# Four of eleven down-projection units by a seven-product block scheme

## The chip, the cores and the metric

The kernel runs on one core of a Trainium2 chip. TensorE multiplies matrices into PSUM, VectorE and ScalarE do elementwise work, GpSimd a little of it, and DMA queues bring the weights in from HBM. The metric is the device time of one execution in microseconds. The profile's rows call the engines PE (TensorE; PEld is its loading of the 128x128 operand that it holds), DVE (VectorE), ACT (ScalarE), POOL (GpSimd) and SP (the queue that issues most DMAs).

## The reference

One layer of a decoder on 256 tokens of width 1024: a mixing block (pooling, an mLSTM and block attention), which the change doesn't touch, and then the feed-forward block:

```python
h2 = rmsnorm(x, ln2_g[l])
u = causal_dwconv(h2 @ w_up[l], ffn_conv[l])              # 1024 -> 2 x 2816
x = x + (jax.nn.silu(u[..., :D_FF]) * u[..., D_FF:]) @ w_down[l]   # 2816 -> 1024
```

The change is in the last product, 256 x 2816 by 2816 x 1024, in float32.

## The kernel before, in words

Every float32 product is made as three matmuls in a shorter type (fp32r). Each operand is split into a *high* part, a copy that ScalarE rounds to fp32r, and a *low* part, the rest, that VectorE gets by a subtraction; the matmuls are high x high, high x low and low x high.

The weights come in *units* of 1 MB (128 partitions x 2048 columns) through a ring of four raw buffers; `load` issues the DMA of the unit four ahead as soon as a unit's split is written in program order, and that DMA waits on the queue until the raw buffer has been read. `split` makes a unit's high part (line 184, ScalarE) and low part (line 191, VectorE) in halves of 1024 columns, into rings of four buffers each (`HL_BUFS`); a half can be written only when TensorE is done with the unit four buffers ago.

The up products (units of the gate and value columns, lines 1110 to 1174) end with one of them per 128 rows of the hidden width: `up_sum`, `up_taps`, `up_gate` and `up_out` leave the gated values, transposed, as `a_hi` and `a_lo`: 22 slabs of 128 rows by 256 tokens. In the program's names raw37 to raw47 are the eleven down units 0 to 10.

The down product has eleven units. Unit i holds 256 rows of `w_down`: two row blocks k = 0, 1 of 128, times 1024 columns, which are two halves c = 0, 1 of 512. The tokens are two blocks t = 0, 1 of 128. So a unit is a 2 x 2 block matrix of tokens (t by k) times a 2 x 2 block matrix of weights (k by c): eight block products, each of three matmuls of 128x128 by 128x512, 24 matmuls in all. Four PSUM accumulators (t, c) collect them over the units. `rows_product` (line 849) writes them.

The order is the order of the program on every engine; nothing is moved later. In the loop from line 1189, unit i's matmuls are written together with the split of unit i + 2. The last two units are kept apart: the four accumulators are finished one after the other, added to the residual `xs` by VectorE (line 1184) and written out, the last one in two tails of 256 columns in other PSUM tiles (`tail`), so that little is left after the last matmul.

Of the kernel before, what the change touches and what calls it, by code (L numbers as in the profile page):

```python
# [26 lines left out]
UMAX = 2080  # L27
RAW_BUFS = 4
# [100 lines left out]
def kernel(  # L129
# [22 lines left out]
    def big(name):  # L152
        return tpool.tile([P, D], F32, tag="big", name=name, bufs=3)
# [7 lines left out]
    def aux(shape, name):  # L161
        return psum.tile(shape, F32, tag="aux", name=name, bufs=4)


    hi_t, lo_t, raw_t = {}, {}, {}

    def unit_cols(u):
        return UMAX if u < N_IN and IN_UNITS[u] in ("vi", "of") else 2048

    def load(u):  # L170
        if u >= N_UNITS:
            return
# [4 lines left out]
        nc.sync.dma_start(raw[:, :n], src)

    def split_hi(u, part, parts):
        if u not in hi_t:  # L180
            hi_t[u] = wpool.tile([P, UMAX], F32R, tag="hi", name=f"hi{u}", bufs=HL_BUFS)
        n = unit_cols(u)
        s = slice(part * n // parts, (part + 1) * n // parts)
        nc.scalar.activation(hi_t[u][:, s], raw_t[u][:, s], AF.Copy)  # L184

    def split_lo(u, part, parts):
        if u not in lo_t:
            lo_t[u] = wpool.tile([P, UMAX], F32R, tag="lo", name=f"lo{u}", bufs=HL_BUFS)
        n = unit_cols(u)
        s = slice(part * n // parts, (part + 1) * n // parts)  # L190
        nc.vector.tensor_sub(lo_t[u][:, s], raw_t[u][:, s], hi_t[u][:, s].bitcast(F32))  # L191
# [26 lines left out]
    for a, b in PARTS:  # L218
        c = slice(KT * (a > 0) + S * a, KT + S * b)
# [18 lines left out]
    def hi_lo(hi, lo, src):  # L238
        nc.scalar.activation(hi, src, AF.Copy)  # L239
        nc.vector.tensor_sub(lo, src, hi.bitcast(F32))  # L240
# [13 lines left out]
    h_2 = cpool.tile([P, KT, 2, S], F32R, name="h_2")  # L254
# [582 lines left out]
    acc = {}  # L837

    def rows_product(u, lhs, kk, first, last, t, cs=(0, 1), ks=(0, 1), sub=(0, 512)):
        hw = hi_t[u][:, :2048].rearrange("p (k c) -> p k c", c=D)  # L840
        lw = lo_t[u][:, :2048].rearrange("p (k c) -> p k c", c=D)
        tok = slice(t * P, (t + 1) * P)
        for k in ks:
            st, sp = first and k == 0, last and k == 1
            lh, ll = lhs[0][:, kk + k, tok], lhs[1][:, kk + k, tok]
            for i, (a, b) in enumerate(((lh, hw), (lh, lw), (ll, hw))):
                for c in cs:
                    o, n = 512 * c + sub[0], sub[1] - sub[0]
                    nc.tensor.matmul(acc[t, c][:, :n], a, b[:, k, o:o + n], start=st and i == 0, stop=sp and i == 2)  # L849
# [22 lines left out]
    for q in range(4):  # L872
        f = [("f", 0), ("f", 1)] if q == 0 else [("f", q + 1)]
# [39 lines left out]
    h = 0  # L913
# [47 lines left out]
    for t in range(NT):  # L961
# [7 lines left out]
        dst = (slice(None), slice(2, 4), slice(t * P, (t + 1) * P))  # L969
# [53 lines left out]
    for n in range(4, n_end):  # L1023
# [30 lines left out]
    up_r, y_t = {}, {}  # L1054
# [88 lines left out]

    def up_gate(i):
        nc.scalar.activation(y_t[i, 0], y_t[i, 0], AF.Silu)  # L1145
        nc.vector.tensor_mul(y_t[i, 1], y_t[i, 0], y_t[i, 1])  # L1146

    def up_out(i):
        hi_lo(a_hi[:, i, :], a_lo[:, i, :], y_t[i, 1])

    for i in range(2, NPAIR + 1):
        u = U_UP + i
        if i == 2:
            up(i, (0,))
            up_rows_t(0)
            up_rows_t(1)
            up(i, (1,))
        elif i < NPAIR:
            up(i)
        for m in (0, 1) if i == 2 else (i - 1,):  # L1160
            if m > 1:
                up_sum(m)
            if i < NPAIR and m:
                split_hi(u + 2, 0, 2)
            up_last(m)
            if i < NPAIR and m:
                split_hi(u + 2, 1, 2)
            if m > 1:
                split_lo(u + 1, 1, 2)
            up_taps(m)  # L1170
            up_gate(m)
            if i < NPAIR and m:
                split_lo(u + 2, 0, 2)
            up_out(m)

    def down(i, t, cs=(0, 1), span=(0, N_DOWN - 1), sub=(0, 512)):
        if i == 0:
            for c in cs:
                acc[t, c] = aux([P, 512], f"dn{t}{c}")
        rows_product(U_DOWN + i, (a_hi, a_lo), 2 * i, i == span[0], i == span[1], t, cs, sub=sub)  # L1180

    def finish(t, c, sub=(0, 512), queue=nc.sync):
        s = slice(c * 512 + sub[0], c * 512 + sub[1])
        nc.vector.tensor_add(xs[:, t, s], acc[t, c][:, :sub[1] - sub[0]], xs[:, t, s])  # L1184
        if queue is not None:
            queue.dma_start(out[t * P:(t + 1) * P, s], xs[:, t, s])

    last = (N_DOWN - 2, N_DOWN - 1)
    for i in range(last[0]):
        down(i, 0)  # L1190
        split(U_DOWN + i + 2, 0)
        down(i, 1, (0,))
        down(i, 1, (1,), (0, last[0] - 1))
        split(U_DOWN + i + 2, 1)
    finish(1, 1, queue=None)
    for i in last:
        down(i, 0)
    for c in range(2):
# [100 lines left out]
```

## Time and profile before

| | us |
|---|---|
| median of 3 runs | 305.64 (305.23 to 306.33) |
| the profiled execution's own time | 305.76 |
| its span, first to last instruction | 304.0 |
| TensorE busy in it | 298.2 |
| VectorE busy | 235.6 |
| ScalarE busy | 196.3 |
| first matmul of the down product starts | 239.56 |
| last addition of a tail starts | 300.73 |

Times in rows are microseconds from the span's start, durations behind them; a group's row has the busy time and the mean duration in ns. An arrow names what ended the idle time ahead of an instruction. Matmul ends are modelled and overlap the next start; a distance between starts is safer. The share of busy time is an average over stages with different limits: VectorE's 77% is 95% of the up stage (105.52 of 111.60 us from 128.0 to 239.6) and 47% of the down stage (28.92 of 61.10 us).

### The profile page before, as it was taken

The page shows a single profiled execution, that of the slowest core. Times are in us where ns is not written, and L with a number is a line of the kernel's source. Part 1 is how long each engine was busy: PE and PEld are TensorE (multiplying, and loading weights), DVE is VectorE, ACT ScalarE, POOL GpSimd, SP SyncE. Part 2 cuts the span into 40 slices and gives each one's busy share as a digit, 9 for nine tenths or more (in the row PEclk, how much of TensorE's full clock was granted, in tenths as well). Part 3 has the DMA queues.
Part 4 walks back from the last instruction along what each step waited for, and adds up shares of the span by engine and source line. Part 5 has one row for each costly group of instructions (what it writes and reads, how often), then busy time and mean ns, then how long its engine had stood idle before and what let it go on. Part 6 is the DMA issues. An engine that isn't in the chain of part 4 may idle for free.

```text
span 304.0 us, 4444 instructions
## 1 busy us (share of the span) xinstructions
PE 298.2 (98%) x1635; PEld 250.6 (82%) x1635; DVE 235.6 (77%) x467; ACT 196.3 (65%) x373; POOL 10.7 (4%) x30
## 2 busy tenths in 40 slices
PE   7999999999999999999999999999999999999995
PEld 3899888788778778888888888888888888888884
DVE  2866999999876667769999999999999986435122
ACT  3775977779995546868777786777877585234000
POOL 1000104510000000000000000000000000000000
PEclk9999999999999999999999999999999999999999
DMA  7999774033337370343563645545456469500003
GB/s 183 394 417 401 307 274 151 2 126 150 123 156 267 149 277 0 140 138 138 160 251 144 227 190 177 240 148 237 170 188 226 141 196 425 208 0 0 0 2 138
DMA packets 9829, 55.20 MB, mean 182 GB/s; under 512 B 1092, under 2 KB 1872, under 8 KB 3920
## 3 DMA queue, kind: packets, MB, share of 16 engines
q1 hardware_dynamic: 9664, 54.79, 48.6%
q8 instruction: 13, 0.21, 0.3%
q10 hardware_dynamic: 144, 0.13, 0.1%
q14 instruction: 8, 0.07, 0.1%
HBM read 53.86 MB, written 1.05 MB: 181 GB/s over the span
## 4 chain that ended last, share of the span: by engine, by line
PE 83%; DVE 7%; DMA 5%; ACT 2%; issue 1%; SPq 1%; ACTq 0%
PE up L1119 24%; PE dn L849 19%; PE up L1120 13%; PE wo L849 7%; DMA raw<-in_w 4%; DVE lo L191 3%; PE of L475 2%; DMA x_t<-in_xt 2%; PE upr L1065 1%; PE V L460 1%; PE upr L1064 1%; PE V L461 1%; PE upr L1066 1%; PE V L462 1%; PE B L460 1%; PE B L462 1%
## 5 line engine op out<-in xcount | busy, mean ns | idle before, releaser
L191 DVE TENSOR_TENSOR lo<-raw,hi 128x1024 fp32r<-128x1024 f32 (+2 forms) x100 | 114.2, 1163 | 24.1 <-ACT hi L184 23.9
L1119 PE MATMUL up<-h,hi 128*128 128x512 f32 x320 | 112.5, 396 | 0.0
L184 ACT ACTIVATE hi<-raw 128x1024 fp32r<-128x1024 f32 (+2 forms) x100 | 97.4, 999 | 21.2 <-PE dn L849 18.0
L1120 PE MATMUL up<-h,lo 128*128 128x256 f32 x320 | 90.1, 282 | 0.0
L1119 PEld LDWEIGHTS up<-h,hi 128*128 128x128 f32 x320 | 60.1, 188 | 14.2 <-DVE z L1127 0.2
L1120 PEld LDWEIGHTS up<-h,lo 128*128 128x128 f32 x320 | 60.2, 188 | 0.0
L1140 DVE SCALAR_TENSOR_TENSOR fy<-z,par,fy 128x255 f32<-128x255 f32 (+1 forms) x80 | 33.2, 476 | 0.0
L849 PE MATMUL dn<-hi,a_lo 128*128 128x512 f32 x84 | 29.5, 394 | 0.0
L849 PE MATMUL dn<-hi,a_hi 128*128 128x512 f32 x84 | 29.4, 393 | 0.0
L849 PE MATMUL dn<-lo,a_hi 128*128 128x512 f32 x84 | 29.4, 393 | 0.0
L1133 ACT ACTIVATE fy<-z,par 128x256 f32<-128x256 f32 x40 | 18.2, 502 | 4.3 <-DVE z L1127 4.3
L849 PEld LDWEIGHTS dn<-lo,a_hi 128*128 128x128 f32 x84 | 15.8, 188 | 3.6
L849 PEld LDWEIGHTS dn<-hi,a_lo 128*128 128x128 f32 x84 | 15.8, 188 | 3.6
L849 PEld LDWEIGHTS dn<-hi,a_hi 128*128 128x128 f32 x84 | 15.7, 188 | 3.6
L1145 ACT ACTIVATE fy<-fy 128x256 f32<-128x256 f32 x22 | 9.2, 418 | 12.5 <-DVE fy L1140 12.4
L239 ACT ACTIVATE a_hi<-fy 128x256 fp32r<-128x256 f32 x22 | 9.2, 418 | 10.8 <-DVE fy L1146 10.8
L1127 DVE TENSOR_TENSOR z<-up,zl 128x512 f32<-128x512 f32 x20 | 13.7, 685 | 0.4 <-ACT zl L1125 0.3
L1184 DVE TENSOR_TENSOR xs<-dn,xs 128x512 f32<-128x512 f32 x4 | 2.7, 688 | 14.0 <-PE dn L849 14.0
L1125 ACT ACTIVATE zl<-up 128x512 f32<-128x512 f32 x20 | 11.7, 585 | 1.7 <-PE up L1120 1.5
L1146 DVE TENSOR_TENSOR fy<-fy,fy 128x256 f32<-128x256 f32 x22 | 9.4, 426 | 3.6 <-ACT fy L1145 2.4
L849 PE MATMUL wo<-hi,mix_hi 128*128 128x512 f32 x32 | 11.1, 409 | 0.0
L849 PE MATMUL wo<-lo,mix_hi 128*128 128x512 f32 x32 | 10.6, 393 | 0.0
(270 smaller groups left out, 469.6 us busy)
## 6 DMA issues: line engine op xcount, KB each, us to landing
raw<-in_w SPq DMA_DIRECT2D x46, 1024.0 KB, 4.8
raw<-in_wg SPq DMA_DIRECT2D x2, 520.0 KB, 6.6
xs<-in_x SPq DMA_DIRECT2D x2, 512.0 KB, 9.7
raw<-in_wg SPq DMA_DIRECT2D x3, 260.0 KB, 5.5
x_t<-in_xt SPq DMA_DIRECT2D x3, 256.0 KB, 5.0
mb<-far SPq DMA_DIRECT2D x1, 768.0 KB, 5.5
out_y<-xs SPq DMA_DIRECT2D x3, 256.0 KB, 2.0
par<-in_params SPq DMA_DIRECT2D x1, 337.0 KB
```

The source lines that it names most:

```text
L184: nc.scalar.activation(hi_t[u][:, s], raw_t[u][:, s], AF.Copy)
L191: nc.vector.tensor_sub(lo_t[u][:, s], raw_t[u][:, s], hi_t[u][:, s].bitcast(F32))
L239: nc.scalar.activation(hi, src, AF.Copy)
L849: nc.tensor.matmul(acc[t, c][:, :n], a, b[:, k, o:o + n], start=st and i == 0, stop=sp and i == 2)
L1119: nc.tensor.matmul(ps[:, j], a, h_2[:, k].rearrange("p c t -> p (c t)"), start=k == 0, stop=False)
L1120: nc.tensor.matmul(ps[:, j, :S], b, h_hi[:, k, :], start=False, stop=k == KT - 1)
L1125: nc.scalar.activation(zl, ps[:, :, S:], AF.Copy)
L1127: nc.vector.tensor_add(z, ps[:, :, :S], zl)
L1133: nc.scalar.activation(y_t[i, j], up_t[i][j], AF.Copy, scale=pcol(Q_FC + i + NPAIR * j + 4 * NPAIR))
L1140: nc.vector.scalar_tensor_tensor(y[:, d:], up_t[i][j][:, :S - d], pcol(Q_FC + i + NPAIR * j + 2 * NPAIR * tap), y[:, d:], op0=ALU.mult, op ...
L1145: nc.scalar.activation(y_t[i, 0], y_t[i, 0], AF.Silu)
L1146: nc.vector.tensor_mul(y_t[i, 1], y_t[i, 0], y_t[i, 1])
```

## The change

For units 2, 4, 6 and 8 the 2 x 2 block product is made from seven block products instead of eight. With token blocks A (t by k) and weight blocks B (k by c) the products are

- M1 = A00 B00 and M2 = A01 B10, on blocks as they are;
- M3 on a difference of token blocks and B11; M4 on A11 and a sum of weight blocks;
- M5, M6 and M7 on differences of token blocks and sums of weight blocks.

M2, M3 and M4 go straight into three of the accumulators that the plain units use. M1 and M5, and M6 and M7, get PSUM tiles of their own, in which they add up over the four units; `combine` puts them together once, after unit 8.

Per such unit VectorE forms four sums of weight blocks (`p13`, `p24`, 2048 columns in three instructions) and four differences of token blocks (`sd`, 512 columns in three), and these get high and low parts as well; of the unit's own blocks only B00, B10 and B11 are still split. The gated values of these units are kept in float32 in a new tile `a_sv`, and the parts of the token differences go into `h_2`, which the up products have done with. A unit of this kind takes two of the four buffers of each ring of high and low parts. The loop prepares a unit when the buffers allow it (`ready`), and the matmuls of unit i are no longer written between the two halves of a split.

Diff, cut to its core:

```diff
+SEVEN = (2, 4, 6, 8)
     def up_gate(i):
         nc.scalar.activation(y_t[i, 0], y_t[i, 0], AF.Silu)
-        nc.vector.tensor_mul(y_t[i, 1], y_t[i, 0], y_t[i, 1])
+        y = a_sv[:, slot[i], :] if i in slot else y_t[i, 1]
+        nc.vector.tensor_mul(y, y_t[i, 0], y_t[i, 1])
+        y_t[i, 1] = y
...
+    def three(dst, a, b, start, stop):
+        for n, (x, y) in enumerate(((0, 0), (0, 1), (1, 0))):
+            nc.tensor.matmul(dst, a[x], b[y], start=start and n == 0, stop=stop and n == 2)
...
+    def down_seven(i):
+        if i == SEVEN[0]:
+            for a, b in ((1, 5), (6, 7)):
+                m = psum_u.tile([P, 2, 2 * S], F32, tag="up", name=f"m{a}{b}", bufs=2)
+                m_t[a], m_t[b] = m[:, 0], m[:, 1]
+            m_t[2], m_t[3], m_t[4] = acc[0, 0], acc[0, 1], acc[1, 0]
+        for n, a, b in ((1, token_block(i, 0, 0), weight_block(i, 0)), (2, token_block(i, 1, 0), weight_block(i, 2)),
+                        (3, diff_block(i, 3), weight_block(i, 3)), (5, diff_block(i, 1), sum_block(i, 0)),
+                        (7, diff_block(i, 0), sum_block(i, 1)), (6, diff_block(i, 2), sum_block(i, 2)),
+                        (4, token_block(i, 1, 1), sum_block(i, 3))):
+            own = n not in (2, 3, 4)
+            three(m_t[n], a, b, own and i == SEVEN[0], own and i == SEVEN[-1])
+
+    def diffs(i):
+        n = SEVEN.index(i)
+        v = a_sv[:, 2 * n:2 * n + 2, :].rearrange("p k (t c) -> p (k t) c", c=P)
+        sd = big(f"sd{i}")
+        d = sd[:, :4 * P].rearrange("p (b c) -> p b c", c=P)
+        nc.vector.tensor_tensor(d[:, 0:2, :], v[:, 1:2, :].to_broadcast([P, 2, P]), v[:, 0:4:3, :], op=ALU.subtract)
+        nc.vector.tensor_sub(d[:, 2, :], v[:, 0, :], d[:, 1, :])
+        nc.vector.tensor_sub(d[:, 3, :], v[:, 2, :], d[:, 2, :])
+        s_hl[i] = [h_2[:, 2 * (n % 4) + x].rearrange("p c t -> p (c t)") for x in range(2)]
+        return sd[:, :4 * P]
+
+    def half_hl(h, l, src, s):
+        nc.scalar.activation(h[:, s], src, AF.Copy)
+        nc.vector.tensor_sub(l[:, s], src, h[:, s].bitcast(F32))
+
+    def sums(i):
...
+        p13 = big(f"p13_{i}")
+        nc.vector.tensor_tensor(p13.rearrange("p (b c) -> p b c", c=512), r[:, 0:4:3, :],
+                                r[:, 1:2, :].to_broadcast([P, 2, 512]), op=ALU.add)
+        p24 = big(f"p24_{i}")
+        nc.vector.tensor_add(p24[:, :512], p13[:, :512], r[:, 3, :])
+        nc.vector.tensor_add(p24[:, 512:], p24[:, :512], r[:, 2, :])
+        d = diffs(i)
+        half_hl(hi_t[u], lo_t[u], raw[:, :512], slice(0, 512))
+        half_hl(hi_t[u], lo_t[u], raw[:, D:], slice(D, 2 * D))
+        hi_lo(*s_hl[i], d)
...
+        half_hl(p_hi[i], p_lo[i], p13, slice(0, D))
+        half_hl(p_hi[i], p_lo[i], p24, slice(D, 2 * D))
+        load(u + RAW_BUFS)
...
+    def combine():
+        x = [[xs[:, t, c * 512:c * 512 + 512] for c in range(2)] for t in range(NT)]
+        m1, v = big("m1")[:, :512], big("mv")[:, :512]
+        nc.scalar.activation(m1, m_t[1], AF.Copy)
+        nc.vector.tensor_sub(v, m_t[6], m1)
+        nc.vector.tensor_add(x[0][0], x[0][0], m1)
+        nc.vector.tensor_add(x[0][1], m_t[5], x[0][1])
+        nc.vector.tensor_add(x[0][1], x[0][1], v)
+        nc.vector.tensor_add(v, m_t[7], v)
+        nc.vector.tensor_add(x[1][1], m_t[5], x[1][1])
+        nc.vector.tensor_add(x[1][1], x[1][1], v)
+        nc.vector.tensor_sub(x[1][0], x[1][0], v)
...
-    for i in range(last[0]):
-        down(i, 0)
-        split(U_DOWN + i + 2, 0)
-        down(i, 1, (0,))
-        down(i, 1, (1,), (0, last[0] - 1))
-        split(U_DOWN + i + 2, 1)
+    pairs = [0]
+    for i in range(N_DOWN):
+        pairs.append(pairs[-1] + 1 + (i in SEVEN))
+    ready = 2
+    for i in range(LAST[0]):
+        while ready < N_DOWN and pairs[ready + 1] - HL_BUFS <= pairs[i]:
+            prepare(ready)
+            ready += 1
+        if i in SEVEN:
+            down_seven(i)
+            if i == SEVEN[-1]:
+                combine()
+        else:
+            down(i, 0)
+            down(i, 1, (0,))
+            down(i, 1, (1,), (0, [n for n in PLAIN if n not in LAST][-1]))
     finish(1, 1, queue=None)
```

By the loop's rule unit 2 is prepared ahead of unit 0's matmuls, unit 3 ahead of unit 1's, units 4 and 5 ahead of unit 3's, 6 and 7 ahead of 5's, 8 and 9 ahead of 7's, and 10 ahead of 8's.

How VectorE's instructions stand at the start of the down stage, before (39 and 40 are units 2 and 3; `waits` names what an instruction waits for):

```order
L240 TENSOR_TENSOR a_lo_1471<-fy211_2638,a_hi_1470 128x256 [waits Activation_49]
L191 TENSOR_TENSOR lo39_2667<-raw39_2506,hi39_2665 128x1024 [waits DMAHW7_49,Activation_49]
L191 TENSOR_TENSOR lo39_2667<-raw39_2506,hi39_2665 128x1024 [waits Activation_49]
L191 TENSOR_TENSOR lo40_2701<-raw40_2563,hi40_2699 128x1024 [waits DMAHW0_49,Activation_49]
L191 TENSOR_TENSOR lo40_2701<-raw40_2563,hi40_2699 128x1024 [waits Activation_49]
```

And after the change (p13 and p24 are sums of weight blocks, sd differences of token blocks, pl the low parts of sums, h_2 the place of the differences' parts):

```order
L1245 TENSOR_TENSOR p13_2_2654<-raw39_2507 128x1024 [waits DMAHW7_49]
L1248 TENSOR_TENSOR p24_2_2656<-p13_2_2654,raw39_2507 128x512 [waits DVE_49]
L1249 TENSOR_TENSOR p24_2_2656<-p24_2_2656,raw39_2507 128x512 [waits DVE_49]
L1228 TENSOR_TENSOR sd2_2659<-a_sv_1472 128x256
L1229 TENSOR_TENSOR sd2_2659<-a_sv_1472,sd2_2659 128x128 [waits DVE_49]
L1230 TENSOR_TENSOR sd2_2659<-a_sv_1472,sd2_2659 128x128 [waits DVE_49]
L1236 TENSOR_TENSOR lo39_2653<-raw39_2507,hi39_2652 128x512 [waits Activation_49]
L1236 TENSOR_TENSOR lo39_2653<-raw39_2507,hi39_2652 128x1024 [waits Activation_49]
L241 TENSOR_TENSOR h_2_103<-sd2_2659,h_2_103 128x512 [waits Activation_49]
L1236 TENSOR_TENSOR pl2_2670<-p13_2_2654,ph2_2669 128x1024 [waits Activation_49]
L1236 TENSOR_TENSOR pl2_2670<-p24_2_2656,ph2_2669 128x1024 [waits Activation_49]
L192 TENSOR_TENSOR lo40_2707<-raw40_2564,hi40_2705 128x1024 [waits DMAHW0_49,Activation_49]
```

Where two instructions of 1024 columns stood for unit 2, eleven stand now, and unit 3's split comes behind them.

TensorE in unit 2 after the change, from its third product (M3, M5, M7, M6 in this order; m15 and m67 are the PSUM tiles of their own):

```order
L1190 MATMUL dn01_2678<-hi39_2652,h_2_103 128x512 [waits Activation_49]
L1190 MATMUL dn01_2678<-lo39_2653,h_2_103 128x512
L1190 MATMUL dn01_2678<-hi39_2652,h_2_103 128x512 [waits DVE_49]
L1190 MATMUL m15_2737<-ph2_2669,h_2_103 128x512 [waits Activation_49]
L1190 MATMUL m15_2737<-pl2_2670,h_2_103 128x512 [waits DVE_49]
L1190 MATMUL m15_2737<-ph2_2669,h_2_103 128x512
L1190 MATMUL m67_2738<-ph2_2669,h_2_103 128x512 [waits PE_49]
L1190 MATMUL m67_2738<-pl2_2670,h_2_103 128x512
L1190 MATMUL m67_2738<-ph2_2669,h_2_103 128x512
L1190 MATMUL m67_2738<-ph2_2669,h_2_103 128x512 [waits Activation_49]
L1190 MATMUL m67_2738<-pl2_2670,h_2_103 128x512 [waits DVE_49]
```

Each product is three matmuls into one PSUM bank in a row, and the second one waits for the low part that VectorE writes.

VectorE at the end, after the change (46 and 47 are units 9 and 10):

```order
L192 TENSOR_TENSOR lo47_2969<-raw47_2861,hi47_2967 128x1024 [waits Activation_49]
L1271 TENSOR_TENSOR mv_2995<-m67_2738,m1_2994 128x512 [waits DVE_49,PE_49,Activation_49]
L1272 TENSOR_TENSOR xs_77<-xs_77,m1_2994 128x512
L1273 TENSOR_TENSOR xs_77<-m15_2737,xs_77 128x512
L1274 TENSOR_TENSOR xs_77<-xs_77,mv_2995 128x512 [waits DVE_49]
L1275 TENSOR_TENSOR mv_2995<-m67_2738,mv_2995 128x512 [waits DVE_49]
L1276 TENSOR_TENSOR xs_77<-m15_2737,xs_77 128x512
L1277 TENSOR_TENSOR xs_77<-xs_77,mv_2995 128x512 [waits DVE_49]
L1278 TENSOR_TENSOR xs_77<-xs_77,mv_2995 128x512
L1282 TENSOR_TENSOR xs_77<-dn11_2698,xs_77 128x512 [waits DVE_49]
L1282 TENSOR_TENSOR xs_77<-dn00_2677,xs_77 128x512 [waits PE_49]
L1282 TENSOR_TENSOR xs_77<-dn01_2678,xs_77 128x512 [waits PE_49]
```

Eight additions have come between the last split and the final additions; before, `dn11` stood right behind the split of unit 10.

More of the change, by code (lines that the diff above doesn't have):

```diff
@@ L1106 @@
     a_lo = fpool.tile([P, NPAIR, S], F32R, name="a_lo")
+    a_sv = fpool.tile([P, 2 * len(SEVEN), S], F32, name="a_sv")
+    slot = {2 * i + k: 2 * n + k for n, i in enumerate(SEVEN) for k in range(2)}
     psum_u = ctx.enter_context(tc.tile_pool(name="psum_u", bufs=2, space=bass.MemoryType.PSUM))
@@ L1174, with matmul, token_block, weight_block @@
             up_out(m)
+    LAST = (N_DOWN - 2, N_DOWN - 1)
+    PLAIN = [i for i in range(N_DOWN) if i not in SEVEN]
+    m_t, p_hi, p_lo, s_hl = {}, {}, {}, {}
+    def matmul(dst, a, b, start, stop):
+        nc.tensor.matmul(dst, a, b, start=start, stop=stop)
+    def three(dst, a, b, start, stop):
+        for n, (x, y) in enumerate(((0, 0), (0, 1), (1, 0))):
+            nc.tensor.matmul(dst, a[x], b[y], start=start and n == 0, stop=stop and n == 2)
+    def token_block(i, k, t):
+        return [d[:, 2 * i + k, t * P:(t + 1) * P] for d in (a_hi, a_lo)]
+    def weight_block(i, n):
+        return [d[U_DOWN + i][:, n * 512:n * 512 + 512] for d in (hi_t, lo_t)]
+    def sum_block(i, n):
+        return [d[i][:, n * 512:n * 512 + 512] for d in (p_hi, p_lo)]
+    def diff_block(i, n):
+        return [d[:, n * P:n * P + P] for d in s_hl[i]]
     def down(i, t, cs=(0, 1), span=(0, N_DOWN - 1), sub=(0, 512)):
@@ new lines, in half_hl @@
+    def half_hl(h, l, src, s):
+        nc.scalar.activation(h[:, s], src, AF.Copy)
+        nc.vector.tensor_sub(l[:, s], src, h[:, s].bitcast(F32))
+    def sums(i):
+        u = U_DOWN + i
+        raw = raw_t[u][:, :2048]
+        r = raw.rearrange("p (b c) -> p b c", c=512)
+        hi_t[u] = wpool.tile([P, UMAX], F32R, tag="hi", name=f"hi{u}", bufs=HL_BUFS)
+        lo_t[u] = wpool.tile([P, UMAX], F32R, tag="lo", name=f"lo{u}", bufs=HL_BUFS)
+        p13 = big(f"p13_{i}")
[8 more added lines that the diff above has]
+        hi_lo(*s_hl[i], d)
+        p_hi[i] = wpool.tile([P, UMAX], F32R, tag="hi", name=f"ph{i}", bufs=HL_BUFS)
+        p_lo[i] = wpool.tile([P, UMAX], F32R, tag="lo", name=f"pl{i}", bufs=HL_BUFS)
+        half_hl(p_hi[i], p_lo[i], p13, slice(0, D))
+        half_hl(p_hi[i], p_lo[i], p24, slice(D, 2 * D))
+        load(u + RAW_BUFS)
@@ new lines, in prepare @@
+    def prepare(i):
+        if i in SEVEN:
+            sums(i)
+        elif i < N_DOWN:
+            split(U_DOWN + i, 0)
+            split(U_DOWN + i, 1)
+    def combine():
[10 more added lines that the diff above has]
+        nc.vector.tensor_sub(x[1][0], x[1][0], v)
@@ L1186, in finish @@
             queue.dma_start(out[t * P:(t + 1) * P, s], xs[:, t, s])
-    last = (N_DOWN - 2, N_DOWN - 1)
-    for i in range(last[0]):
-        down(i, 0)
-        split(U_DOWN + i + 2, 0)
-        down(i, 1, (0,))
-        down(i, 1, (1,), (0, last[0] - 1))
-        split(U_DOWN + i + 2, 1)
+    pairs = [0]
[6 more added lines that the diff above has]
+            ready += 1
+        if i in SEVEN:
+            down_seven(i)
[5 more added lines that the diff above has]
+            down(i, 1, (1,), (0, [n for n in PLAIN if n not in LAST][-1]))
     finish(1, 1, queue=None)
-    for i in last:
+    for i in LAST:
         down(i, 0)
@@ L1199 @@
         finish(0, c)
-    for i in last:
+    for i in LAST:
         down(i, 1, (0,))
@@ L1204 @@
         acc[1, 1] = psum_u.tile([P, 2, 2 * S], F32, tag="up", name=f"tail{h}", bufs=2)[:, 0]
-        for i in last:
-            down(i, 1, (1,), last, sub)
+        for i in LAST:
+            down(i, 1, (1,), LAST, sub)
         finish(1, 1, sub, queue)
```

## The prediction

> **What bounds the kernel now.** I read the engine totals first, then the chain that ended last, then the last stage alone. "Unit 2" and so on are the eleven down units; a *plain* unit is one in eight products, a *seven* unit (2, 4, 6, 8 after the change) one in seven.
>
> ```profile
> span 304.0 us, 4444 instructions
> PE 298.2 (98%) x1635; PEld 250.6 (82%) x1635; DVE 235.6 (77%) x467; ACT 196.3 (65%) x373; POOL 10.7 (4%) x30
> ```
> TensorE (PE) is busy for 98% of the span. The chain of waits in order of time says the same of the last stage:
> ```profile
> 239.72 58.19 PE dn L849 x252
> 297.90 2.80 PE tail L849 x24
> 300.73 0.42 DVE xs L1184
> ```
> From 239.7 us on nothing but matmuls stands in the chain, until one addition of 0.42 us. So a matmul taken out there is worth what it occupies. That is not its duration in the page (393 ns), because they overlap; it is the distance from start to start, from the first and the last rows of the stage in the timeline:
> ```profile
> 239.56 0.63 PE L849 MATMUL dn<-hi,a_hi 128*128 128x512 f32 x2
> ...
> 242.33 0.39 PE L849 MATMUL dn<-hi,a_hi 128*128 128x512 f32 x1
> 242.56 0.39 PE L849 MATMUL dn<-lo,a_hi 128*128 128x512 f32 x1
> ...
> 297.74 0.28 PE L849 MATMUL tail<-hi,a_hi 128*128 128x256 f32 x1
> ```
> 252 matmuls of 512 columns lie between 239.56 and 297.74: 0.2309 us each. Where matmuls alternate between two PSUM banks (239.56 to 242.33 is twelve of them) and where they go to one bank in a row (242.33 to 242.56) the pace is the same 0.23. A plain unit takes 24 x 0.2309 = 5.54 us.
>
> The other engines have room, and this stretch of the windows view says how much:
> ```profile
> core 0: us, PE busy (x) PEld busy (x) DVE busy (x) ACT busy (x) POOL busy (x), PEclk, DMA share, GB/s
> 239.60:300.70 61.10, 61.09 (x277) 50.04 (x276) 28.92 (x33) 20.10 (x23) 0.00 (x0) 1.00 0.33 125
> ```
> VectorE (DVE) is busy for 28.9 of 61.1 us, ScalarE (ACT) for 20.1, GpSimd for nothing, at a granted clock of 1.00. The whole question is whether VectorE can take the added work inside what is left.
>
> **The change, part by part.**
>
> *Removed: matmuls.* Four units go from 24 to 21 matmuls: 12 x 0.2309 = 2.77 us, all on the path. The waits in the new rows of TensorE are more numerous (eleven or twelve in a seven unit, four in a plain one); the plain units' waits leave no mark on the 0.23 pace, so I cost a wait that is already met at nothing.
>
> *Added: VectorE's work.* These rows give the prices (one by form, the rest from the timeline):
> ```profile
> L191 DVE TENSOR_TENSOR lo<-raw,hi 128x1024 fp32r<-128x1024 f32 x20 | 23.4, 1220 | 15.8 <-ACT hi L184 15.8
> 244.84 0.42 DVE L240 TENSOR_TENSOR a_lo<-fy,a_hi 128x256 fp32r<-128x256 f32 x1 [0.49 <-ACT a_hi L239]
> 257.48 2.36 DVE L191 TENSOR_TENSOR lo<-raw,hi 128x1024 fp32r<-128x1024 f32 x2 [2.52 <-ACT hi L184]
> 289.63 0.69 DVE L1184 TENSOR_TENSOR xs<-dn,xs 128x512 f32<-128x512 f32 x1 [7.62 <-PE dn L849]
> 294.94 1.29 DVE L1184 TENSOR_TENSOR xs<-dn,xs 128x512 f32<-128x512 f32 x2 [4.62 <-PE dn L849]
> 34.07 1.51 DVE L503 SCALAR_TENSOR_TENSOR mqT<-mqz,par,mqT 128x255 f32<-128x255 f32 x3
> L503 DVE SCALAR_TENSOR_TENSOR mqT<-mqz,par,mqT x6: 466/482/484, 34.1 to 40.0; 128x255 f32<-128x255 f32 x2, 128x254 f32<-128x254 f32 x2, 128x253 f32<-128x253 f32 x2
> ```
> An operation of 1024 columns lasts 1.22 us, and the next one starts 2.36 - 1.22 = 1.14 after it; for 512 columns 0.69 and 0.60 (1.29 - 0.69); for 256 columns 0.42. From 256 to 1024 columns that is 1.04 ns a column, so 128 columns are an estimate of 0.29, with 0.21 to the next start. Where an operation needs the one just before it, it starts after that one's end: three dependent ones of 0.48 take 1.51, so 0.515 each, 0.03 above the duration.
>
> A seven unit is eleven operations in VectorE's order, as steps from start to start: weight sums 1.25 (its follower needs it), 0.72, 0.60; token differences 0.45, 0.31, 0.21; low parts 0.60 (512 columns), 1.14, 0.60 (differences), 1.14, 1.14. Sum 8.16 us, against 2.28 for a plain unit. The two together are 10.44 us on VectorE and 45 x 0.2309 = 10.39 on TensorE. They are practically level, so the spare time at the first seven unit decides.
>
> *Where VectorE starts.* Its last a_lo starts at 244.84, and the first weight sum needs only data loaded long ago: 244.84 + 0.34 = 245.18. Unit 2 starts on TensorE at 239.56 + 48 x 0.2309 = 250.64. The tightest product is its eleventh, which needs the low part of the first pair of sums: it starts at 245.18 + 5.88, is there at 252.28, and is wanted at 250.64 + 10 x 0.2309 = 252.95. Spare 0.67 us. The seventeenth product, with the second pair: there at 253.42, wanted at 254.33, spare 0.91. Each period of a seven and a plain unit eats 0.05, so unit 8 has 0.52 left. Hence the formula of this prediction: if each seven unit costs VectorE e us more than 8.16, TensorE loses about 4e - 0.52, and nothing while e is under 0.13. Of units 9 and 10, VectorE finishes at 245.18 + 4 x 8.16 + 5 x 2.28 = 289.22; their low parts are in time by over 1 us.
>
> *ScalarE.* It gives the high parts.
> ```profile
> 244.72 5.78 ACT L184 ACTIVATE hi<-raw 128x1024 fp32r<-128x1024 f32 x6
> 256.39 2.01 ACT L184 ACTIVATE hi<-raw 128x1024 fp32r<-128x1024 f32 x2 [3.58 <-PE dn L849]
> ```
> Six in 5.78 us are 0.95 each. A period is five of them and two of half size, under 6 of 10.4 us. In each seven unit it copies the differences 3.62 us after VectorE's first sum and the sums by 4.2 to 6.2; VectorE wants them at 5.28, 5.88 and 7.02. The 3.58 us shows ScalarE waiting for a buffer that TensorE frees. With four such buffers, unit 8's sums take those of unit 6, which is done at 239.56 + 159 x 0.2309 = 276.3; ScalarE wants them at 245.18 + 3 x 10.44 + 4.2 = 280.7.
>
> *Loads.* A seven unit gives its raw buffer free 5.4 us after its first sum, not after 2.
> ```profile
> L177 SPq DMA_DIRECT2D raw<-in_w x46: 327/328/362, 7.2 to 259.9; - x46
> ...
> DMA to landing us min/median/max: 4.7/4.8/12.5
> ```
> Unit 8's load follows unit 4's sums: 255.62 + 5.4 + 4.8 = 265.8, wanted at 276.5. Nothing on the path; with a landing of 12.5 it would still be in time.
>
> *The end.* Eight more additions come behind 289.22. Three wait for their predecessor: 5 x 0.60 + 3 x 0.72 = 5.16, so 294.38. What is queued behind them are all the final additions: dn11, dn00, dn01, dn10 at 0.60 each, so the first tail addition can start at 296.78 and the last at 297.12. TensorE now frees the last one at 300.73 - 2.77 = 297.96: spare 0.84. The PSUM tile that the first tail matmul wants (294.97) is read out by 293.2. The outputs bunch: the first is issued at about 295.7 as before, the last 2.8 us earlier.
> ```profile
> 295.66 5.85 SPq L1186 DMA_DIRECT2D out_y<-xs  x4
> out_y<-xs SPq DMA_DIRECT2D x3, 256.0 KB, 2.0
> 297.00:298.00 1.00, 1.00 (x7) 0.82 (x6) 0.06 (x1) 0.00 (x0) 0.00 (x0) 1.00 0.92 344
> ```
> The first two are issued 0.6 us apart already and still land in 2.0 us, which speaks for no delay; at worst the last 128 KB waits for the 128 KB ahead of it, 0.4 us at the 344 GB/s of that microsecond. I take 0.1.
>
> *Sum.* The profiled execution took 305.76 us (span 304.0), 0.12 above the median of 305.64. 305.76 - 2.77 = 302.99; +0.1 for the outputs; and for e.
>
> *What no row shows:* an addition of two parts of one tile, one of them with a repeated operand. The nearest row of a repeated operand, L574, costs as much as a plain one of 256 columns, which puts e at nothing:
> ```profile
> L574 DVE TENSOR_TENSOR knA<-A,akr x2: 414/419/424, 52.9 to 53.2; 128x256 f32<-128x256 f32 x2
> 35.42 1.11 POOL L638 TENSOR_SCALAR_AFFINE_SELECT mb<-mb 128x1024 f32<-128x1024 f32 x1 [33.29 <-DMA mb<-far]
> 35.50 3.24 DVE L191 TENSOR_TENSOR lo<-raw,hi 128x1024 fp32r<-128x1024 f32 x2
> ```
> The upper end is the slowest pair of two-operand additions in this trace: 3.24 instead of 2.36, 0.44 more per 1024 columns, at a time when GpSimd works, which it doesn't in the last stage. On the 2560 columns of new additions that is e = 1.1. Below nothing brings nothing, since TensorE then paces. I take e = 0.15, close to L574: 4 x 0.15 - 0.52 = 0.08. Forecast 303.17; 303.2.
>
> A rule against this change: the Trainium skill, VectorE: DVE Perf Modes, "The DRAIN you can't avoid", says that the next operation does not start until the pipe is empty. Every step would then be a full duration. The trace disagrees (2.36 us for two of 1.22), and the page's next section lets an operation that isn't held start earlier; what it would make of the time is rival 2.
>
> **The rivals.**
>
> 1. *VectorE paces the stage.* With e of 0.3 to 0.6 (a few hundredths at each of the eleven waits) TensorE stands still in every seven unit from unit 4 on: 4e - 0.52 is 0.7 to 1.9 us, 303.8 to 305.0, at e = 0.5 304.6. For it: 10.44 against 10.39 leaves no reserve. Against it: each price comes from a row of the same stage or the same operation.
>
> 2. *No overlap of VectorE's operations.* With 0.69, 1.22 and 0.29 for every 0.60, 1.14 and 0.21, a seven unit is 8.75, a plain one 2.44, the work up to 289.22 takes 3.16 longer and the nine steps of 512 columns behind it 0.81; less the spare 0.84 that is 3.13, and with the 0.1 306.2: no change. Against it stands the 2.36. It is what the Trainium skill's rule would give.
>
> 3. *Slower: the new additions run slower than those known.* One mechanism, in the three weight sums and three differences of each seven unit: both operands come out of one tile, in strides of blocks. At 0.44 per 1024 columns e = 1.1, TensorE loses 3.9 us, 307.0. The change is slower from e = 1.0 on. For it: only the row at 35.50. Against it: L574, and that row's GpSimd. The Trainium skill, Vector Engine (DVE) Microarchitecture Reference, "Measured stream behaviour on trn2", has full rate wherever runs of two or more words are adjacent; no run here shows that yet.
>
> That the change doesn't do what it says I leave out: the order of instructions has the 21 matmuls.
>
> **How the numbers follow.** Forecast 0.58 (302.7 to 303.6), rival 1 0.26, rival 2 0.07, rival 3 0.09. A measurement of this kernel tells 0.3%, 0.92 us, from no change: faster is below 304.72. The forecast and two thirds of rival 1 (e under 0.54) lie there: 0.58 + 0.17 = 0.75. Within: 0.09 + 0.07 = 0.16. Slower: rival 3, 0.09. The range reaches over the forecast and rival 1: from 302.6 (e at nothing, no bunching, and the runs' own spread) to 305.3.
>
> **What would show it.** Right: 1623 matmuls, at 0.23 us; TensorE without idle time between 250 and 287 us; the weight sum at 1.22 us; VectorE without a gap from 245.2 to about 297, the last addition at 298.0 to 298.2. VectorE's units (first sum to first sum of the next seven unit) near 10.4 us. Rival 1: TensorE waits in seven units for `pl` from VectorE, longer at each, and periods of 10.7 to 11. Rival 2: two splits in 2.44 instead of 2.36, and tail additions that wait for VectorE. Rival 3: a weight sum of 1.6 us. I am wrong altogether if TensorE waits for ScalarE, a load or a buffer.

## The result and the profile after

The changed kernel takes 303.44 us (median of 4 runs, 303.25 to 303.63) against 305.88 us (4 runs, 305.23 to 306.33) for the kernel before in the same comparison: a ratio of 0.9922, with a 95% interval of 0.9901 to 0.9942. On a second chip it was 303.19 us (6 runs) against 305.45 us (11 runs), 0.9920 (0.9905 to 0.9936). It is faster by 0.8%. The forecast was 303.2, in a range of 302.6 to 305.3.

The profiled execution took 303.43 us. The engine totals of the changed kernel:

```profile
span 301.2 us, 4485 instructions
PE 295.4 (98%) x1623; PEld 248.3 (82%) x1623; DVE 263.1 (87%) x511; ACT 204.7 (68%) x386; POOL 10.7 (4%) x30
```

Twelve matmuls have gone, and VectorE has 27.5 us more of work (263.1 - 235.6). The chain of waits of the changed kernel, its end in order of time:

```profile
281.86 0.70 PE m L1190 x3
282.56 1.38 PE dn L1190 x6
283.94 2.08 PE m L1190 x9
286.02 0.70 PE dn L1190 x3
286.72 8.31 PE dn L850 x36
295.03 2.80 PE tail L850 x24
297.83 0.02 issue
297.85 0.42 DVE xs L1282
```

It is TensorE all the way, as before, and the matmuls of a seven unit run at the old pace: 9 in 2.08 us are 0.231 each. The windows view of the changed kernel, for the whole last stage and for the stretch in which the four seven units lie:

```profile
core 0: us, PE busy (x) PEld busy (x) DVE busy (x) ACT busy (x) POOL busy (x), PEclk, DMA share, GB/s
239.60:298.20 58.60, 58.22 (x264) 47.65 (x263) 56.40 (x78) 28.32 (x36) 0.00 (x0) 1.00 0.35 127
...
250.00:287.00 37.00, 37.00 (x161) 1.00 0.40 142
```

VectorE, which was busy for half of this stage before, now is for 56.4 of 58.6 us. TensorE has no idle time at all from 250 to 287. Two engines are full, and only one of them sets the time.

VectorE's timeline shows the eleven operations of unit 2 and, behind them, the split of unit 3 and the first sum of unit 4; then the end of the stage:

```profile
244.71 0.42 DVE L241 TENSOR_TENSOR a_lo<-fy,a_hi 128x256 fp32r<-128x256 f32 x1 [0.48 <-ACT a_hi L240]
245.05 1.22 DVE L1245 TENSOR_TENSOR p<-raw 128x1024 f32<-128x1024 f32 x1
246.30 0.69 DVE L1248 TENSOR_TENSOR p<-p,raw 128x512 f32<-128x512 f32 x1
...
248.62 1.82 DVE L1236 TENSOR_TENSOR lo<-raw,hi 128x512 fp32r<-128x512 f32 x2
250.36 0.68 DVE L241 TENSOR_TENSOR h<-sd,h 128x512 fp32r<-128x512 f32 x1
250.97 2.35 DVE L1236 TENSOR_TENSOR pl<-p,ph 128x1024 fp32r<-128x1024 f32 x2
253.24 2.35 DVE L192 TENSOR_TENSOR lo<-raw,hi 128x1024 fp32r<-128x1024 f32 x2
255.51 1.22 DVE L1245 TENSOR_TENSOR p<-raw 128x1024 f32<-128x1024 f32 x1
...
282.33 2.35 DVE L1236 TENSOR_TENSOR pl<-p,ph 128x1024 fp32r<-128x1024 f32 x2
284.60 4.63 DVE L192 TENSOR_TENSOR lo<-raw,hi 128x1024 fp32r<-128x1024 f32 x4
289.14 0.68 DVE L1271 TENSOR_TENSOR mv<-m,m 128x512 f32<-128x512 f32 x1
...
296.71 0.41 DVE L1282 TENSOR_TENSOR xs<-tail,xs 128x256 f32<-128x256 f32 x1
297.85 0.42 DVE L1282 TENSOR_TENSOR xs<-tail,xs 128x256 f32<-128x256 f32 x1 [0.73 <-PE tail L850]
```

A seven unit is 253.24 - 245.05 = 8.19 us on VectorE, a seven and a plain unit together 255.51 - 245.05 = 10.46. TensorE's timeline gives the other side, the tightest product of the first and of the last seven unit:

```profile
239.42 0.63 PE L850 MATMUL dn<-hi,a_hi 128*128 128x512 f32 x2
...
252.79 0.39 PE L1190 MATMUL m<-pl,h 128*128 128x512 f32 x1
...
284.01 0.39 PE L1190 MATMUL m<-pl,h 128*128 128x512 f32 x1
284.24 0.63 PE L1190 MATMUL m<-ph,h 128*128 128x512 f32 x2
```

In unit 2 the low part of the sums is there at 250.97 + 1.22 = 252.19 and its matmul starts at 252.79, 0.60 us later. In unit 8 it is 283.55 against 284.01: 0.46. The reserve shrinks by 0.05 at each seven unit, and it lasts. But these differences overstate it. The wait for a low part stands on the weight load ahead of the matmul, as the first experiment shows, and that load starts one matmul earlier (PEld's timeline at the same two places):

```profile
252.56 0.19 PEld L1190 LDWEIGHTS m<-pl,h 128*128 128x128 f32 x1
...
283.78 0.19 PEld L1190 LDWEIGHTS m<-pl,h 128*128 128x128 f32 x1
```

Up to the load, 0.37 us are left in unit 2 and 0.23 in unit 8.

**Where the time went.** I measure the last stage from its first matmul to the start of the last addition. It was 300.73 - 239.56 = 61.17 us and is 297.85 - 239.42 = 58.43: 2.74 less. The profiled executions differ by 305.76 - 303.43 = 2.33. The difference is made of four pieces: the stage (-2.74), its start (239.42 for 239.56, -0.14), the stretch behind the last addition's start (3.35 for 3.27, +0.08), and the time outside the span, which the trace doesn't cover (303.43 - 301.2 = 2.23 for 1.76, +0.47). Spans are given to 0.1 us, so the last two pieces are good to about 0.05. The last one was not foreseen, and it comes back below.

### The profile page after: what moved, and what is told of

The parts are those of the page before. It is cut to its first block, busy times and chain, and to the rows that moved or that the text cites. A ratio compares the mean times of both kernels' runs of the same rounds, so it can differ in the third digit from the quotient of the medians.

```text
span 301.2 us, 4485 instructions
## 1 busy us (share of the span) xinstructions
PE 295.4 (98%) x1623; PEld 248.3 (82%) x1623; DVE 263.1 (87%) x511; ACT 204.7 (68%) x386; POOL 10.7 (4%) x30
## 4 chain that ended last, share of the span: by engine, by line
PE 81%; DVE 7%; DMA 6%; ACT 2%; SPq 1%; issue 1%; ACTq 0%
PE up L1122 25%; PE up L1123 13%; PE dn L850 12%; PE wo L850 8%; DMA raw<-in_w 4%; PE m L1190 4%; DVE lo L192 3%; PE dn L1190 3%; DMA raw<-in_wg 2%; PE upr L1066 1%; PE V L461 1%; PE upr L1065 1%; PE V L463 1%; PE upr L1067 1%; PE V L462 1%; PE B L461 1%
## 5 line engine op out<-in xcount | busy, mean ns | idle before, releaser
L192 DVE TENSOR_TENSOR lo<-raw,hi 128x1024 fp32r<-128x1024 f32 (+2 forms) x92 | 104.9, 1157 | 8.0 <-ACT hi L185 7.9
L185 ACT ACTIVATE hi<-raw 128x1024 fp32r<-128x1024 f32 (+2 forms) x92 | 89.5, 995 | 3.1 <-DMA raw<-in_w 1.5
L850 PE MATMUL dn<-hi,a_hi 128*128 128x512 f32 x52 | 18.2, 394 | 0.0
L850 PE MATMUL dn<-hi,a_lo 128*128 128x512 f32 x52 | 18.2, 394 | 0.0
L850 PE MATMUL dn<-lo,a_hi 128*128 128x512 f32 x52 | 18.1, 392 | 0.0
L850 PEld LDWEIGHTS dn<-lo,a_hi 128*128 128x128 f32 x52 | 9.8, 188 | 2.3
L850 PEld LDWEIGHTS dn<-hi,a_lo 128*128 128x128 f32 x52 | 9.8, 188 | 2.2
L850 PEld LDWEIGHTS dn<-hi,a_hi 128*128 128x128 f32 x52 | 9.7, 188 | 2.2
L850 PE MATMUL wo<-hi,mix_lo 128*128 128x512 f32 x32 | 10.6, 393 | 0.0
L240 ACT ACTIVATE a_hi<-fy 128x256 fp32r<-128x256 f32 x14 | 5.9, 418 | 6.9 <-DVE fy L1150 6.9
```

## The experiments

The theory: TensorE paces the stage, each matmul taken out is worth 0.231 us, and VectorE keeps up with some tenths of a us to spare. The rivals that the result left open: that VectorE is already what paces (a smaller price per addition would then bring more), that part of the gain was paid back by the additions, the eight additions at the end, or the outputs. Because the stage's start moves by up to 1 us between profiles (239.0 to 240.0), I compare the stage's own length and give the medians beside it.

### One more addition in each seven unit

```diff
+    extra = fpool.tile([P, 512], F32, name="extra")
...
         d = diffs(i)
+        nc.vector.tensor_add(extra[:, :128], raw[:, 512:512 + 128], raw[:, D:D + 128])
```

The added operation uses the raw block and its result goes nowhere. The first kernel adds 128 columns:

> The changed kernel with one more addition of 128 columns on VectorE in each seven unit, right behind the token differences, into a tile that nobody reads. Theory (VectorE runs level with TensorE, and the tightest product of unit 8 had 0.46 us left in the profile after): each such addition is a step of 0.21, four of them 0.84, TensorE loses 0.84 - 0.46 = 0.4 us against the changed kernel, near 303.8, and it stands still for about that in units 6 and 8 only, waiting for a low part of the sums. Rival A (VectorE has room, as its share of busy time would have it): no idle time of TensorE, no loss. Rival B (VectorE sets the pace already): 0.8 us lost, with idle time from unit 2 on.

The second adds 512 columns in the same place:

> The same with 512 columns, a step of 0.60. Theory: 4 x 0.60 - 0.46 = 1.9 us lost against the changed kernel, near 305.4, TensorE standing still first in unit 4 and then 0.6 us in each seven unit. Rival A (room): no loss, 303.4. Rival B (no spare time left): 2.4 us, 305.8.

Measured with 128 columns: 304.07 us (6 runs) against 305.40 for the kernel before (23 runs), ratio 0.9952 (0.9937 to 0.9967); the stage is 298.94 - 240.00 = 58.94 us, 0.51 longer than the changed kernel's. With 512 columns: 305.41 us (12 runs), ratio 0.9995 (0.9984 to 1.0006), stage 300.25 - 239.71 = 60.54, 2.11 longer. In the median the whole gain is gone with one addition of 512 columns per unit. The stage is still 0.63 us shorter than before the change. What makes up for that is the stretch behind the last addition's start (304.0 - 300.25 = 3.75 us, 3.27 before) and 0.1 us more outside the span. So it is partly luck that the median hits the expected 305.4.

The chain of the kernel with 128 columns more, where units 4, 6 and 8 have their nine matmuls on the sums:

```profile
263.68 2.12 PE m L1191 x9
...
274.12 2.32 PE m L1191 x9
...
284.81 2.29 PE m L1191 x9
```

They were 2.08 in the changed kernel. The list of waits of that kernel (the engine and line that waits, what it waits for; us in total, times, longest) has the cause, and the one of the kernel with 512 columns has more of it:

```profile
PEld m L1191 <- DVE pl L1237: 1.0, 3, 0.4
```

```profile
PEld m L1191 <- DVE pl L1237: 1.9, 4, 0.5
PEld dn L1191 <- DVE lo L1237: 1.4, 3, 0.5
```

The changed kernel has no wait of TensorE in this stage. So with these additions VectorE begins to pace, for the operand that the prediction named, `pl`, and with 512 columns for `lo` too. But the stalls begin one seven unit earlier than I expected: in unit 4 with 128 columns (I had said 6 and 8 only), and with 512 columns in unit 2, where the load at 253.13 waited 0.33 us (I had said unit 4). The losses of 0.51 and 2.11 are above the formula's 0.4 and 1.9 as well. The low part of unit 8 in the kernel with 128 columns, the three weight loads that waited, and unit 8's matmuls show why:

```profile
283.72 2.35 DVE L1237 TENSOR_TENSOR pl<-p,ph 128x1024 fp32r<-128x1024 f32 x2
```

```profile
263.67 0.19 PEld L1191 LDWEIGHTS m<-pl,h 128*128 128x128 f32 x1 [0.20 <-DVE pl L1237]
...
274.33 0.19 PEld L1191 LDWEIGHTS m<-pl,h 128*128 128x128 f32 x1 [0.41 <-DVE pl L1237]
...
284.99 0.19 PEld L1191 LDWEIGHTS m<-pl,h 128*128 128x128 f32 x1 [0.37 <-DVE pl L1237]
```

```profile
284.99 0.50 PE L1191 MATMUL m<-pl,h 128*128 128x512 f32 x1
285.32 0.63 PE L1191 MATMUL m<-ph,h 128*128 128x512 f32 x2
```

The low part is there at 283.72 + 1.22 = 284.94, the weight load starts 0.05 later, and the matmul behind the stalled one starts 0.33 behind the load. In the changed kernel, undisturbed, it starts 0.46 behind it (283.78 and 284.24). So a load can be about 0.13 us late at no cost, and a stall costs less than the wait listed for it: the three waits are 0.98 us together, and the nine matmuls took 0.04, 0.24 and 0.21 longer than 2.08, 0.49 in all. Both kernels give the same reserve. VectorE's period went from 10.46 to 10.66 and 11.06 us, and 4 x 0.20 - 0.51 and 4 x 0.60 - 2.11 are both 0.29 us. Unit 8's rows in the changed kernel come to about the same: 0.23 up to the load, less the 0.05, plus the 0.13.

### The matmuls put back, the additions kept

```diff
-                        (4, token_block(i, 1, 1), sum_block(i, 3))):
+                        (4, token_block(i, 1, 1), sum_block(i, 3)), (4, token_block(i, 1, 1), sum_block(i, 3))):
```

> The changed kernel with the product M4 issued twice in each seven unit: all the added work on VectorE and ScalarE, 24 matmuls in every unit as before. M4 is counted twice in the output. Theory (the gain is the 12 matmuls and nothing else): 2.77 us above the changed kernel, 306.2, within 0.3% of the kernel before, and TensorE never idle in the stage. Rival (part of the gain comes from the other order of splits and matmuls): under 305.5. Rival (the added work costs something that the saved matmuls cover): over 306.8.

Measured: 306.08 us (12 runs), ratio 1.0023 (1.0012 to 1.0033). The windows view of this kernel and the ends of its stage:

```profile
239.50:300.70 61.20, 61.10 (x277) 50.04 (x276) 56.43 (x78) 28.44 (x36) 0.00 (x0) 1.00 0.35 125
```

```profile
239.45 0.63 PE L850 MATMUL dn<-hi,a_hi 128*128 128x512 f32 x2
...
300.64 0.42 DVE L1282 TENSOR_TENSOR xs<-tail,xs 128x256 f32<-128x256 f32 x1 [0.97 <-PE tail L850]
```

The stage is 61.19 us, as long as before the change (61.17), with VectorE's load of after (56.4 us). Twelve matmuls more are 61.19 - 58.43 = 2.76 us, and VectorE's additions beside them cost 0.02. With 24 matmuls in every unit VectorE has more time than in the changed kernel, so this run gives the price of the matmuls; what the additions cost at the changed kernel's pace is the next experiment. The median is 0.68 above that of before all the same. Its median span is 303.95 us against 303.7, its time outside the span 2.15 against 1.71.

### The additions dropped, the matmuls as changed

```diff
+        p13, p24 = raw[:, :D], raw[:, D:]
```

and the differences replaced by the token blocks themselves; six operations of each seven unit go.

> The changed kernel without the weight sums and the token differences: the high and low parts are made straight from the raw blocks and the gated values, so the products are of other blocks than they should be, and their number and shapes stay. VectorE has 3.6 us less to do in each seven unit. Theory (the additions are hidden altogether): the same time within 0.2 us of the changed kernel, 303.2 to 303.5; only the final additions come earlier. Rival (VectorE costs something on the path): 0.5 us or more below it.

Measured: 302.89 us (6 runs), ratio 0.9915 (0.9900 to 0.9929). This is 0.55 below the changed kernel's 303.44 and 0.30 below its 303.19 on the second chip, lower than I expected, and against the first of the two it reaches the rival's mark of 0.5. But 0.26 of it is time outside the span (1.89 for 2.15), and the stage speaks against the rival. It is 297.56 - 239.13 = 58.43 us, to the hundredth what it is with the additions. VectorE's timeline of this kernel shows that it had room again:

```profile
261.43 0.69 DVE L1231 TENSOR_TENSOR lo<-raw,hi 128x512 fp32r<-128x512 f32 x1 [2.29 <-ACT hi L1230]
...
297.56 0.42 DVE L1272 TENSOR_TENSOR xs<-tail,xs 128x256 f32<-128x256 f32 x1 [0.97 <-PE tail L850]
```

It waits 2.29 us for ScalarE there, where the changed kernel has no gap, and TensorE doesn't get faster by it. That VectorE already paces the changed kernel is refuted.

### The additions at the end dropped

```diff
             down_seven(i)
-            if i == SEVEN[-1]:
-                combine()
```

> The changed kernel without the final combination: M1, M5, M6 and M7 are never added to the output. Eight additions of 512 columns on VectorE and a copy on ScalarE are gone from the end. Theory (they are hidden, and all that they cost is that four outputs are issued within 1.6 us): 0.0 to 0.2 us below the changed kernel, and outputs land in 2.0 instead of up to 2.4 us. Rival (the end of VectorE's queue is on the path): 0.5 us or more.

Measured: 303.00 us (6 runs), ratio 0.9923 (0.9909 to 0.9937); the stage is 58.44 us. The median is 0.44 and 0.19 below the changed kernel's two, and 0.35 less time outside the span (1.80 for 2.15) accounts for most of that. The eight additions cost nothing in the stage, as the 0.73 us of waiting ahead of the last addition in the changed kernel already says. The stretch behind the start of the last addition is 3.28 us without them, 3.27 before the change and 3.35 with them. With spans given to 0.1 us, a bunching of the outputs by 0.1 is neither shown nor excluded. The output of 128 KB that took 2.4 us to land with the additions took 1.9 without them, near the 2.0 expected, but another one took 3.7.

### Three and five units by seven products

```diff
-SEVEN = (2, 4, 6, 8)
+SEVEN = (2, 4, 6)
```

with the eight additions of the end moved behind unit 8's matmuls, and

```diff
-SEVEN = (2, 4, 6, 8)
+SEVEN = (2, 4, 6, 7, 8)
```

> Units 2, 4 and 6 by seven products, unit 8 plain; the final combination stays behind unit 8. Theory: three matmuls more than the changed kernel, 0.69 us, near 304.1, and VectorE with 5.9 us of idle time. Rival (four seven units are already too many for VectorE): faster than or level with the changed kernel.

> Units 2, 4, 6, 7 and 8 by seven products: three matmuls less (0.69 us), 5.9 us more on VectorE. Theory (VectorE has no room for a fifth): unit 7's low parts come 2.9 us late and unit 8's another 2.4, TensorE ends its units about 5.3 us later than in the changed kernel, 308.7, slower than before by 2.8. Rival (room by the share of busy time): 302.7.

Five: 308.71 us (4 runs), ratio 1.0109 (1.0093 to 1.0125), the expected 308.7. The stage is 303.56 - 239.50 = 64.06 us, 5.63 longer than the changed kernel's, though three more matmuls are gone. I had expected 5.3, and 0.43 less time outside the span (1.72 for 2.15) helped the median, so the exact hit is luck. TensorE's timeline in units 7 and 8 of the version with five:

```profile
278.54 0.50 PE L1190 MATMUL m<-lo,a_hi 128*128 128x512 f32 x1 [1.97 <-DVE lo L1236]
...
286.73 0.50 PE L1190 MATMUL m<-lo,a_hi 128*128 128x512 f32 x1 [1.26 <-DVE lo L1236]
```

Without a plain unit between them, seven units ask 8.2 us of VectorE for 4.85 us (21 x 0.231) of TensorE. The stall isn't at the sums: VectorE works in order, and when it is late already the unit's first low part is what TensorE wants first.

Three: the stage is 298.15 - 239.01 = 59.14 us, 0.71 longer, which is the three matmuls more (0.69). But the median of 303.23 us (6 runs, ratio 0.9935, 0.9918 to 0.9952) missed the expected 304.1. So I ran it again beside the changed kernel, on another chip:

> The changed kernel as it is, beside the kernel with three seven units on one chip. Theory: its stage, from the first matmul of the down product to the last tail addition, takes 58.4 us again, and its median is 0.7 us below that of three seven units and 2.7 to 2.8 below the kernel before. Rival (the saved matmuls are partly lost elsewhere): level with three seven units.

> Units 2, 4 and 6 by seven products once more, beside the changed kernel. Theory: the stage takes 59.1 us, 0.7 more than in the changed kernel; what the whole time differed less by in the other comparison was the start of the stage, which lay between 239.0 and 240.0 us in the profiles of all kernels, whatever their down product.

Three again: 303.39 us (6 runs), ratio 0.9931 (0.9915 to 0.9947), stage 59.13. Changed again: 303.19 us, stage 58.43. The stages differ by 0.70 each time, the medians by only 0.20. The difference lies in two pieces that aren't the stage. The median spans are 301.6 and 301.0, 0.6 apart. The time outside the span is 1.79 and 2.16, 0.37 apart in the other direction.

### The differences on GpSimd

```diff
-        nc.vector.tensor_tensor(d[:, 0:2, :], v[:, 1:2, :].to_broadcast([P, 2, P]), v[:, 0:4:3, :], op=ALU.subtract)
-        nc.vector.tensor_sub(d[:, 2, :], v[:, 0, :], d[:, 1, :])
-        nc.vector.tensor_sub(d[:, 3, :], v[:, 2, :], d[:, 2, :])
+        nc.gpsimd.tensor_tensor(d[:, 0:2, :], v[:, 1:2, :].to_broadcast([P, 2, P]), v[:, 0:4:3, :], op=ALU.subtract)
+        nc.gpsimd.tensor_sub(d[:, 2, :], v[:, 0, :], d[:, 1, :])
+        nc.gpsimd.tensor_sub(d[:, 3, :], v[:, 2, :], d[:, 2, :])
```

> The three token differences of each seven unit on GpSimd instead of VectorE, the rest as changed. VectorE has 0.97 us less per seven unit. Theory (VectorE slows while GpSimd works, 0.88 us for 1.11 us in the pair at 35.50 us of the profile before): GpSimd takes about 1.5 us per unit, VectorE loses 1.2 of it, its weight sums last 1.5 to 2.0 us instead of 1.22, a seven unit is 0.2 longer than 8.19, and the time is 0.3 to 0.5 us above the changed kernel. Rival (no contention, the long pair had another cause): weight sums at 1.22, a seven unit of 7.2 us, the same time as the changed kernel since TensorE paces.

Measured: 303.24 us (6 runs), ratio 0.9929 (0.9914 to 0.9945), stage 58.44: no change, where a loss was expected. The slowing that I expected is there, though. VectorE's and GpSimd's timelines of this kernel, at units 2 and 4:

```profile
244.68 1.48 DVE L1245 TENSOR_TENSOR p<-raw 128x1024 f32<-128x1024 f32 x1
...
255.80 1.11 DVE L1248 TENSOR_TENSOR p<-p,raw 128x512 f32<-128x512 f32 x1
```

```profile
245.15 1.32 POOL L1230 TENSOR_TENSOR sd<-a_sv,sd 128x128 f32<-128x128 f32 x1
252.50 3.86 POOL L1228 TENSOR_TENSOR sd<-a_sv 128x256 f32<-128x256 f32 x1 [6.03 <-DVE pl L1236]
```

Where the two engines work at once, VectorE's sum takes 1.48 us instead of 1.22, or that of 512 columns 1.11 instead of 0.69; GpSimd's difference of 256 columns takes between 1.00 and 3.92 us, where the same size on GpSimd took 0.73 to 0.75 earlier in the kernel before (GpSimd's durations in a profile are rough). Not every operation is slowed: the sum of 1024 columns at 254.55, with GpSimd's 3.86 us beside it, took the usual 1.22. VectorE's three periods are 9.87, 10.85 and 9.88 us, 10.20 in the mean. Of the 0.97 us that left VectorE in each seven unit it kept 0.26, and since TensorE paces, that 0.26 is worth nothing.

## Why the prediction was right

- **Removed matmuls.** 2.77 was forecast for the path, the stage became 2.74 shorter, and putting the twelve back cost 2.76. That waits already met leave no mark on TensorE's pace was right too.
- **VectorE's prices.** A seven unit came to 8.19 against 8.16, the period to 10.46 against 10.44, the start to 245.05 against 245.18 (the stage itself starts 0.14 earlier). The weight sum, strided and with one operand repeated, took 1.22 us, so e, what a seven unit costs beyond 8.16, was about 0.03, not the 0.15 taken. Two of 1.22 still take 2.35.
- **The reserve.** This term was mis-sized. Forecast were 0.67 at unit 2 and 0.52 at unit 8, and to the matmul's start it is 0.60 and 0.46. But the prediction took the matmul's start for the time at which the low part is wanted, and the wait stands on the weight load, 0.23 earlier; with the 0.13 that a late load makes up again, the reserve was 0.29. The slope of the formula 4e - 0.52 was right: 0.2 us more per unit lost 0.51 us, 0.6 more lost 2.11, which is 1.60 for 4 x 0.40. Its threshold was too high.
- **Rival 1** was closer than the formula had it (0.13): by the 0.29 over four units, an estimate, VectorE is about 0.07 us per seven unit away from pacing, a third of an addition of 128 columns. The profile of before couldn't have told this without the sum step by step; the busy share of half left the impression of much room.
- **Rival 2** falls by the pair in 2.35 and the 0.73 us wait of the last addition. **Rival 3** falls by the 1.22 (its own sign was 1.6). The Trainium skill, Vector Engine (DVE) Microarchitecture Reference, "Measured stream behaviour on trn2", had full rate for such strides; these sums, in runs of 512 words, agree.
- **The end.** Preparations were done at 289.14 (forecast 289.22), the first tail addition at 296.71 (296.78), the last waits for TensorE as forecast, the stretch behind the last addition's start grew by 0.08 (0.1), which is within the rounding of the spans.
- **ScalarE, loads and buffers.** No wait of TensorE for any of them.

What the sum missed is the part that it left alone: 305.76 - 304.0 = 1.76 us outside the span was carried over unchanged, and became 2.23. It was partly offset by the stage's start, 0.14 earlier, and by an e taken too high, so it is partly luck that the total of 303.17 lies this near to the 303.44; with e at 0.03 the forecast would have been 303.09. The reserve taken too high did no harm only because e was small. My later expectations missed too: the stalls with one addition more began a seven unit earlier, and the median without the additions came out lower than I said. The two plain misses were three seven units, where the median came out 0.9 us lower than I said, 0.4 of it by this time outside the span and the rest by the spread of the stage's start and of the runs, and GpSimd, where I took a slowed VectorE for a loss without setting it against the work that had left it.

## What to carry to other kernels

When work moves from the engine that paces to one with idle time, set the two engines' periods against each other, start to start and operation by operation, and work out the spare at the first unit and at the last: here 10.46 against 10.39 us was enough for four units, and five, two of them next to each other, lost 5.6 us. Count the spare to the instruction that waits, here the weight load and not its matmul: 0.37 us at unit 2 and not 0.60. What the change is worth is then the matmuls alone, at their distance from start to start (0.231 us, not the 0.39 of their duration). For effects of half a us compare a stage's own length in the traces as well as the medians, because the start of the stage and the time outside the span move by as much.

## What was not expected

**The time outside the span** (a run's time less its core's span) comes mostly in two levels, about 0.4 us apart (the kernel with the additions dropped lies between). Which one a run has goes by kernel more than by chip; three seven units show both. The lowest, median and highest of each kernel's runs:

```
                         us outside the span     runs
before (second chip)     1.69  1.72  1.75        11
changed                  2.13  2.15  2.23         4
changed, again           2.12  2.16  2.33         6
matmuls put back         2.12  2.15  2.23        12
differences on GpSimd    2.17  2.25  2.32         6
128 columns more         1.77  1.83  1.92         6
512 columns more         1.77  1.83  1.97        12
additions dropped        1.71  1.89  2.00         6
end additions dropped    1.70  1.80  1.85         6
five seven units         1.68  1.72  1.75         4
three seven units        1.75  1.79  2.31         6
three, again             1.76  1.79  2.35         6
```

It doesn't follow the number of matmuls or of additions, or the outputs: the kernel with 128 columns more has every instruction of the changed one and lies low. It took 0.44 us of the gain (the median span fell by 2.7 us on the second chip, the median time by 2.26), and it is the reason why three seven units nearly match four. What sets it is not covered by any trace here and stays open.

**The granted clock** fell in the middle of a stage. In the version with five seven units TensorE stands still for 2 us ahead of 278.54, the longest such gap in these kernels' last stages; its four runs have a mean clock of 0.993 or 0.994, all others 0.997 or more. The windows view of TensorE in that version, by the microsecond:

```profile
277.00:278.00 1.00, 0.00 (x0) 1.00 0.00 0
...
279.00:280.00 1.00, 0.94 (x4) 0.62 0.00 0
280.00:281.00 1.00, 1.00 (x3) 0.50 0.00 0
...
282.00:283.00 1.00, 1.00 (x5) 0.67 0.00 0
283.00:284.00 1.00, 1.00 (x6) 1.00 0.00 0
```

From about 279.24 to 282.66 the clock is halved, by the 0.62 and 0.67 of the microseconds at the two ends. The gap of 1.26 us at 286.73 has no such effect. The Trainium skill, TensorE: Matmul & The Clock Gate, "The HAM clock gate (the "warmup" mystery)", has the clock halved after an idle window of about 3.4 us; here a gap of 2 us was enough, and the clock was back after about 3.4 us. It cost nothing in this version, since VectorE sets the time there: the chain of waits runs through VectorE without a break up to 289.56, and a TensorE at full clock would only have waited longer at 286.73. In a stage that TensorE paces, a stall of that length would cost more than its own time: 3.4 us at half the clock are 1.7 us of matmuls, an estimate from these rows that no run here shows.
